# A transformer layer's sparse experts on one core: loads held back, unread products in a gap, and token weights computed later

## The chip, the cores and the metric

The kernel runs on one core of one Trainium2 chip. The metric is the device time of one execution in microseconds, taken as the median of several runs. A time "at 505.30" is microseconds from the start of the profiled span. TensorE's clock has two levels here, 1.2 and 2.4 GHz; the profile gives the granted clock as a share of the higher one, so 0.50 is the lower level and 1.00 the higher.

## The reference

Two layers (`DEPTH = 2`) over 512 tokens of width 1024, float32. Each has a token mixer (attention) and then a sparse mixture of 16 experts, of which every token uses two. The change lies in the experts:

```
def _moe(h, w_router, router_bias, w_gate, w_up, w_down):
    scores = jax.nn.sigmoid((t @ w_router).astype(jnp.float32))
    sel = scores + router_bias.astype(jnp.float32)
    grp_score = jnp.sum(lax.top_k(sel.reshape(-1, N_GROUPS, EXPERTS_PER_GROUP), TOP_K)[0], -1)
    best = jnp.argmax(grp_score, axis=-1)
...
    _, idx = lax.top_k(jnp.where(in_group, sel, -jnp.inf), TOP_K)
    top_s = jnp.take_along_axis(scores, idx, axis=-1)
    gate = top_s / jnp.sum(top_s, -1, keepdims=True)
    combine = jnp.sum(jax.nn.one_hot(idx, N_EXPERTS, dtype=jnp.float32) * gate[..., None], 1)
    hg = jnp.einsum('td,edf->tef', t, w_gate)
    hu = jnp.einsum('td,edf->tef', t, w_up)
    act = jax.nn.silu(hg) * hu * combine[..., None].astype(t.dtype)
    y = jnp.einsum('tef,efd->td', act, w_down)
```

`w_gate` and `w_up` are 1024x256 for each expert, `w_down` 256x1024.

## The kernel before, in words

The instructions of each engine stand in one fixed order, in which the engine runs them; waits between engines are semaphores that the framework puts in. `tc.issue_after(x)` puts what is built inside it behind instruction x in that order. Loads are asked for on SP's queue unless another engine is named, and a load waits until its tile's last reader is done.

**Products.** A float32 product is made of three passes over split operands: H is the operand rounded to the matmul format (a cast on ScalarE, `wH`, L215), L the rest (a subtraction on VectorE, `wL`, L216), and TensorE adds H·H, L·H and H·L (L225 to L227). `wH` and `wL` have six buffers each (`NWH`), each holds 128x512 and serves six products of 128x256.

**The router.** For each layer the last norm of the mixer gives `h` (512 tokens); its four 128-row tiles go to `h2d` in DRAM, three from SP's queue and the last from ScalarE's (L996). VectorE ranks the scores in many small operations; small matmuls count positions (`pos`) and turn the ranking into lists of token rows (`mp`, L1088). `vt` (L1093) holds the row numbers that the gathers and scatters use. Then VectorE computes the token weights: `rt_tmp`, `posf`, `rt_den`, `rt_gt` (L1098 to L1106) and, in `keep_weights`, `rt_we` (L1207 to L1210) and `ae` (L1214), which TensorE transposes (L1215) into `G`, for the last two experts (`NKEEP`).

**The experts.** For each expert e, in order: `x_load` gathers its up to 128 token rows from `h2d` into `xe` by an indirect DMA on POOL (L1119); `x_split` transposes them on TensorE (eight of 128x128, L330) and splits them into `xH` (ScalarE, L337) and `xL` (VectorE, L338); `x_gate` makes 24 products and a silu (`ea`, L1144), `x_up` 24 more; `x_down` (L1188) is issued one expert later, behind the next gate, and its result `ye` is scattered by POOL (L1193). `overflow()` stands between the first gather and the first split: a branch that all engines take and whose body runs only if an expert has more than 128 tokens.

**What is loaded ahead.** `AHEADW` lists twelve weight tiles of 1 MB, those of experts 0 to 3. The first `HOLD` of them are asked for on SP early, from the end of the mixer on, as their buffers come free; the others on POOL, behind gather 0. Before the change HOLD is 10: only (3, up) and (3, down) wait for the gather. The three `xes` are the gathers' buffers, which ScalarE clears (L1028) once in each layer.

Of the kernel before, what the change touches and what calls it, by code (L numbers as in the profile page):

```python
# [13 lines left out]
OP = mybir.AluOpType  # L14
# [73 lines left out]
def build(tc, A, out):  # L88
    nc = tc.nc
    with ExitStack() as es:  # L90
# [90 lines left out]
        xdr = dr.tile([S, D], F32, name="xdr")  # L181


        def wraw(src, shape, tag="raw", eng=SY):
            if tag in ("f4", "row"):
                n = 1024 // shape[1]
                raws = [(fp if tag == "f4" else rp).tile([P, n] + shape[1:], F32, tag=tag, name="raw4") for _ in range(shape[0] // n)]
                for i, raw in enumerate(raws):
                    eng.dma_start(raw, src[:, i * n:(i + 1) * n])
                return lambda s: raws[s.start // n][:, s.start % n:s.start % n + s.stop - s.start]  # L190
            raw = wp.tile([P] + shape, F32, tag="raw", name="raw", bufs=NRAW) if tag == "raw" else e8("raw8", shape)
            eng.dma_start(raw, src)
# [107 lines left out]
        def stats(src):  # L300
            st = small("st", [2, 6])
            for i in range(2):
                V.bn_stats(st[:, i, :], parts(src, i * 512, (i + 1) * 512)[0][0])
            mv = small("mv", [2])
            V.bn_aggr(mv, st.rearrange("p a b -> p (a b)"))
            r = pool_rsqrt("rstd", mv[:, 1:2], LN_EPS, 1)
            nb = small("nb", [1])
            PO.tensor_scalar(nb, mv[:, 0:1], r, -1.0, op0=OP.mult, op1=OP.mult)
            return mv[:, 0:1], r, nb

        issued = {}

        def norm(src, name, g, b, st=None):

            m, r, nb = st or stats(src)
            n = f4(name, [D])
            for lo, hi in ((0, 256), (256, D)):
                for p, z in parts(src, lo, hi):
                    V.scalar_tensor_tensor(n[:, z], p, m, g[:, z], op0=OP.subtract, op1=OP.mult)
            V.scalar_tensor_tensor(n, n, r, b, op0=OP.mult, op1=OP.add)  # L320
            return n

        def plain(src, dst, st=None):

            m, r, nb = st or stats(src)
            ACT.activation(dst, src, AF.Identity, bias=nb, scale=r)

        def turn(dst, src):
# [93 lines left out]
        def layer(l, hH, hL, W0, after=None, qk=None):  # L422
# [660 lines left out]
            for k in range(2):  # L1083
                for t in range(NT):
                    at = ats[:, NT * k + t]
                    V.tensor_scalar(at, iotab, sv[:, 0, k, t:t + 1], None, op0=OP.is_equal)
                    for i in range(2):
                        PE.matmul(mp, lhsT=at, rhs=src[:, NT * k + t, 2 * i:2 * i + 2], start=(k == 0 and t == 0 and i == 0),  # L1088
                                  stop=(k == 1 and t == NT - 1 and i == 1))
            cnti = small("cnti", [1], I32, bufs=1)  # L1090
            V.tensor_reduce(cnti, pos[:, NT, :], axis=X, op=OP.max)
            vt = small("vt", [2, NE], I32, bufs=1)
            order1 = V.tensor_tensor(vt, ct["none"].rearrange("p (i e) -> p i e", i=2), mp, op=OP.subtract)  # L1093
            vidx, tidx = vt[:, 0], vt[:, 1]
# [7 lines left out]
            den = rt("den", [NT])
            V.tensor_add(den, sv[:, 1, 0, :], sv[:, 1, 1, :])
            V.reciprocal(den, den)
            gt = rt("gt", [2, NT])
            V.tensor_mul(gt, sv[:, 1], den[:, None, :].to_broadcast([P, 2, NT]))  # L1106
            gm = rt("gm", [2, NT])
            V.tensor_scalar(gm, sv[:, 0], float(CAP), None, op0=OP.is_lt)
# [15 lines left out]
            def x_split(e):  # L1124
                xe = XE.pop(e)
                xH = f4("xH", [8, P], F32R)
                xL = f4("xL", [8, P], F32R)
                for q in range(2):
                    p = ptp([P, 4, P])
                    transposes(lambda i: xe[:, (4 * q + i) * P:(4 * q + i + 1) * P], p, 4)  # L1130
                    split_ps(p, xH[:, 4 * q:4 * q + 4, :], xL[:, 4 * q:4 * q + 4, :])
                XS[e] = xH, xL

            def x_prod(e, w):
                xH, xL = XS[e]
# [147 lines left out]
                            V.tensor_copy(oi[:, 0:n], sh[:, 0:n])  # L1283

            for e in range(AHEAD):
                i = x_load(e)
                if e == 0:
                    first = i
            with tc.issue_after(first.ins):
                for e, w, tag in AHEADW[HOLD:]:  # L1290
                    PRE[e, w] = wraw(x_src(e, w), x_shape(w), tag, PO)
            overflow()
            x_split(0)
            for e in range(NE):
                if e + AHEAD < NE:
                    x_load(e + AHEAD)
                if e == EKEEP:
                    keep_weights()
                x_gate(e)
                if e > 0:  # L1300
                    x_down(e - 1)
                x_up(e)
                if e + 1 < NE:
                    x_split(e + 1)
            ys = []
            for t in range(NT):
                for k in range(2):
# [106 lines left out]
```

## Time and profile before

| | |
|---|---|
| median of 3 runs | 1373.92 us (1373.52 to 1374.74) |
| the profiled execution's own time | 1374.85 us |
| its span | 1373.1 us |
| mean granted TensorE clock over the span | 0.961 |
| TensorE busy | 1262.8 us (92%) |
| VectorE busy | 1031.9 us (75%) |
| ScalarE busy | 704.5 us (51%) |
| GpSimd (POOL) busy | 157.5 us (11%) |
| moved by DMA | 263.59 MB, mean 192 GB/s |

The profiled execution is one of the kernel's executions, 0.93 us above the median; 1.75 us of its time lie outside the span. Busy shares are averages over stages with different limits: of the table TensorE's 92% tells only that the other 8% are where it stands still. The experts of layer 1 begin at about 499 us, those of layer 2 at about 1162 us.

### The profile page before, as it was taken

The page shows a single profiled execution, that of the slowest core. Times are in us where ns is not written, and L with a number is a line of the kernel's source. Part 1 is how long each engine was busy: PE and PEld are TensorE (multiplying, and loading weights), DVE is VectorE, ACT ScalarE, POOL GpSimd, SP SyncE. Part 2 cuts the span into 40 slices and gives each one's busy share as a digit, 9 for nine tenths or more (in the row PEclk, how much of TensorE's full clock was granted, in tenths as well). Part 3 has the DMA queues.
Part 4 walks back from the last instruction along what each step waited for, and adds up shares of the span by engine and source line. Part 5 has one row for each costly group of instructions (what it writes and reads, how often), then busy time and mean ns, then how long its engine had stood idle before and what let it go on. Part 6 is the DMA issues. An engine that isn't in the chain of part 4 may idle for free.

```text
span 1373.1 us, 21373 instructions
## 1 busy us (share of the span) xinstructions
PE 1262.8 (92%) x7925; PEld 1027.6 (75%) x7925; DVE 1031.9 (75%) x2104; ACT 704.5 (51%) x1460; POOL 157.5 (11%) x161
## 2 busy tenths in 40 slices
PE   4898999999999949999969899999999994999996
PEld 3787777677778948888648777777777794788883
DVE  4877788776368879999886888564325978799997
ACT  2344444556644157777434454455556413777760
POOL 1032000000000222222020300000000012222210
PEclk9799999999999969999988999999999997899999
DMA  9747544455156187999643365112123546889963
GB/s 309 235 138 292 174 152 166 149 189 184 62 170 224 59 303 261 311 336 342 249 157 131 114 224 177 46 60 70 50 77 111 179 156 218 274 281 342 351 221 136
DMA packets 181070, 263.59 MB, mean 192 GB/s; under 512 B 18281, under 2 KB 131337, under 8 KB 180960
## 3 DMA queue, kind: packets, MB, share of 16 engines
q1 hardware_dynamic: 157104, 221.27, 47.8%
q0 software_dynamic: 11456, 24.07, 5.0%
q10 hardware_dynamic: 12400, 16.83, 3.8%
q8 instruction: 64, 1.05, 0.3%
q14 instruction: 46, 0.38, 0.1%
HBM read 250.79 MB, written 27.30 MB: 203 GB/s over the span
## 4 chain that ended last, share of the span: by engine, by line
PE 32%; DVE 10%; ACT 2%; issue 2%; DMA 2%; POOL 1%; SPq 1%; POOLq 0%; DVEq 0%; ACTq 0%
PE mm L225 5%; PE mm L226 5%; PE mm L227 5%; DVE wL L216 5%; PE mm L1188 3%; PE tp L330 2%; PE av L668 1%; PE y L1321 1%; ACT wH L215 1%; POOL rs L286 1%; PE mo L226 1%; PE mo L227 1%; PE mo L225 1%; PE s L634 1%; DMA raw<-in_w_exp_down 1%
## 5 line engine op out<-in xcount | busy, mean ns | idle before, releaser
L216 DVE TENSOR_TENSOR wL<-raw,wH 128x512 fp32r<-128x512 f32 x520 | 339.7, 685 | 94.4 <-ACT wH L215 80.6
L215 ACT CAST wH<-raw 128x512 fp32r<-128x512 f32 x520 | 318.4, 622 | 163.5 <-PE mm L1188 45.9
L225 PE MATMUL mm<-hH,wH 128*128 128x512 f32 x544 | 219.3, 403 | 0.0
L226 PE MATMUL mm<-hL,wH 128*128 128x512 f32 x544 | 217.9, 400 | 0.0
L227 PE MATMUL mm<-hH,wL 128*128 128x512 f32 x544 | 216.1, 397 | 0.0
L225 PE MATMUL mm<-wH,xH 128*128 128x256 f32 x512 | 149.1, 291 | 2.6 <-DVE yk L1189 1.6
L227 PE MATMUL mm<-wH,xL 128*128 128x256 f32 x512 | 148.6, 290 | 1.0 <-DVE xL L338 1.0
L226 PE MATMUL mm<-wL,xH 128*128 128x256 f32 x512 | 146.4, 286 | 0.3 <-DVE wL L216 0.3
L226 PEld LDWEIGHTS mm<-hL,wH 128*128 128x128 f32 x544 | 103.4, 190 | 21.9 <-issue 2.1
L225 PEld LDWEIGHTS mm<-hH,wH 128*128 128x128 f32 x544 | 103.2, 190 | 21.8 <-issue 0.8
L227 PEld LDWEIGHTS mm<-hH,wL 128*128 128x128 f32 x544 | 103.4, 190 | 21.2 <-issue 0.7
L249 DVE SCALAR_TENSOR_TENSOR acc<-araw,cond,acc 128x512 f32<-128x512 f32 x148 | 110.5, 747 | 5.7 <-DMA araw<-in_w_ada 3.0
L225 PEld LDWEIGHTS mm<-wH,xH 128*128 128x128 f32 x512 | 98.8, 193 | 5.5 <-DVE yk L1189 2.5
L226 PEld LDWEIGHTS mm<-wL,xH 128*128 128x128 f32 x512 | 98.6, 193 | 2.4 <-DVE wL L216 1.2
L227 PEld LDWEIGHTS mm<-wH,xL 128*128 128x128 f32 x512 | 98.2, 192 | 2.3 <-DVE xL L338 1.8
L286 POOL TENSOR_TENSOR rstd<-rstd,c_mhalf 128x1 f32<-128x1 f32 x32 | 20.4, 637 | 478.1 <-DVE rstd L285 478.1
L642 ACT ACTIVATE pp<-s,nm,rs 128x512 f32<-128x512 f32 x64 | 49.7, 778 | 33.0 <-DVE nm L639 31.3
L1188 PE MATMUL mm<-raw,eT 128*128 128x512 f32 x128 | 63.3, 617 | 3.6 <-ACT eT L1171 1.5
L225 PE MATMUL mm<-wH,hH 128*128 128x256 f32 x192 | 58.7, 308 | 5.4 <-ACT hH L406 3.6
L227 PE MATMUL mm<-wH,hL 128*128 128x256 f32 x192 | 57.2, 303 | 1.6 <-DVE hL L372 1.4
L1193 POOL DMA_INDIRECT y<-ye,vt x28 | 33.6, 1199 | 210.1 <-DVE ye L1189 210.1
L226 PE MATMUL mm<-wL,hH 128*128 128x256 f32 x192 | 56.7, 299 | 0.0
(303 smaller groups left out, 2655.7 us busy)
## 6 DMA issues: line engine op xcount, KB each, us to landing
araw<-in_w_ada SPq DMA_DIRECT2D x44, 1024.0 KB, 5.4
raw<-in_w_in SPq DMA_DIRECT2D x40, 1024.0 KB, 5.1
raw<-in_w_exp_gate SPq DMA_DIRECT2D x32, 1024.0 KB, 9.1
raw<-in_w_exp_up SPq DMA_DIRECT2D x28, 1024.0 KB, 11.1
raw<-in_w_exp_down SPq DMA_DIRECT2D x28, 1024.0 KB, 9.4
raw<-in_w_out SPq DMA_DIRECT2D x8, 1024.0 KB, 5.3
y<-y SPq DMA_DIRECT2D x16, 512.0 KB, 8.1
eraw<-in_w_ada SPq DMA_DIRECT2D x4, 1024.0 KB, 13.8
```

The lines of the kernel that those rows point to most:

```text
L215: ACT.copy(H, raw(s))
L216: V.tensor_sub(L, raw(s), H.bitcast(F32))
L225: PE.matmul(o, lhsT=lH, rhs=rH, start=(i == 0), stop=False)
L226: PE.matmul(o, lhsT=lH, rhs=rL, start=False, stop=False)
L227: PE.matmul(o, lhsT=lL, rhs=rH, start=False, stop=(i == n - 1))
L249: last = V.scalar_tensor_tensor(acc, raw[:, k, :], ck, acc, op0=OP.mult, op1=OP.add)
L286: PO.tensor_tensor(r, r, mhalf[:, :n], op=OP.pow)
L330: return PE.transpose(dst, src, ident[0:k, 0:k])
L634: PE.matmul(s, lhsT=qT[h // 4][:, h % 4, tcols(t)], rhs=kTH[:, kv, :], start=True, stop=False)
L642: ACT.activation(pp, s, AF.Exp, bias=nm, scale=rs, accum_out=dn)
L1188: PE.matmul(p, lhsT=a, rhs=w, start=(i == 0), stop=(i == len(todo) - 1))
L1193: st = PO.indirect_dma_start(out=y2, out_offset=bass.IndirectOffsetOnAxis(ap=vidx[:, e:e + 1], axis=0), in_=ye, in_offset=None, bounds_che ...
```

## The change

Four things change, and one small one besides.

1. HOLD goes from 10 to 4. Only (0, gate), (0, up), (0, down) and (1, gate) are asked for early. The other eight tiles, in the same order, are asked for on SP behind the branch of `overflow()` (`load_held`). Ahead of the first of them ScalarE copies one column of `mp` into its tile, so that the DMA, which writes the same tile, waits for the copy and so for `mp`; the second half of that weight and the rest follow.
2. Seven matmuls of 128x512 (`idle`, bfloat16) that nobody reads are put on TensorE behind the last matmul of `mp`, ahead of expert 0's transposes.
3. The token weights (`token_weights`) and `keep_weights` are built behind the last `xL` of expert 1's rows instead of right behind `vt`.
4. With that the scheduler places the last `h2d` tile's DMA on ScalarE behind one more clearing of an `xe` buffer.

The small one: `nb`, a scalar per token that only `plain` needs, is computed there and no longer in each `stats`. Line numbers after the change are a few higher than before: `ae` is L1222 instead of L1214, its transposes L1223 instead of L1215, the products L229 to L231 instead of L225 to L227.

```
+            with tc.issue_after(last.ins):
+
+                idle = pat([P, 512], "idle")
+                for i in range(NIDLE):
+                    last = PE.matmul(idle, lhsT=oneb, rhs=ats[:, 0:4], start=(i == 0), stop=(i == NIDLE - 1))
+            warm = last
...
-            with tc.issue_after(order1.ins):
+            def token_weights():
+
                 V.tensor_mul(tmp, o12, sco[:, None].to_broadcast([P, 2, NT, NE]))
-                posf = rt("posf", [NT + 1, NE])
                 V.tensor_copy(posf, pos)
-            V.reduce_sum(sv[:, 1], tmp, axis=X)
...
+                V.reduce_sum(sv[:, 1], tmp, axis=X)
...
             for e in range(AHEAD):
-                i = x_load(e)
-                if e == 0:
-                    first = i
-            with tc.issue_after(first.ins):
+                x_load(e)
+
+            def load_held():
+
+                hold = None
                 for e, w, tag in AHEADW[HOLD:]:
-                    PRE[e, w] = wraw(x_src(e, w), x_shape(w), tag, PO)
+                    with ExitStack() as order:
+                        if hold is not None:
+                            order.enter_context(tc.issue_after(hold.ins))
+                        PRE[e, w] = wraw(x_src(e, w), x_shape(w), tag, first=None if hold else lambda z: ACT.copy(z, mp[:, 0, 0:1]))
+                    hold = hold or issued["load"]
+
             overflow()
-            x_split(0)
+            load_held()
+            with tc.issue_after(warm.ins):
+                split1 = x_split(0)
             for e in range(NE):
                 if e + AHEAD < NE:
                     x_load(e + AHEAD)
                 if e == EKEEP:
-                    keep_weights()
+                    with tc.issue_after(split1.ins):
+                        token_weights()
+                        keep_weights()
...
                 if e + 1 < NE:
-                    x_split(e + 1)
+                    i = x_split(e + 1)
+                    split1 = i if e == 0 else split1
...
-HOLD = 10
+HOLD = 4
+NIDLE = 7
```

VectorE behind `vt`, before the change: the token weights and the first four `rt_we` operations, then the branch of `overflow()` (`cnti`).

```order
L1093 TENSOR_TENSOR vt<-c_none,mp 128x32
L1098 TENSOR_TENSOR rt_tmp<-rt_o_4912,rt_sco 128x128
L1100 COPY rt_posf<-pos 128x80
L1101 TENSOR_REDUCE rt_sv<-rt_tmp 128x8
L1103 TENSOR_TENSOR rt_den<-rt_sv 128x4
L1104 RECIPROCAL rt_den<-rt_den 128x4
L1106 TENSOR_TENSOR rt_gt<-rt_sv,rt_den 128x8
L1207 TENSOR_TENSOR rt_we<-rt_o_4912,rt_gt 128x8
L1208 TENSOR_TENSOR rt_we<-rt_we,rt_gm 128x8
L1209 TENSOR_TENSOR rt_gt<-rt_gt,rt_we 128x8
L1210 TENSOR_TENSOR rt_we<-rt_we 128x4
L1220 TENSOR_LOAD cnti
```

After the change the branch follows `vt` at once, and these operations stand among the subtractions of experts 1 and 2. VectorE's order from right behind the last subtraction of (2, gate), over the four of (2, up), which read raw_5084, to the second group of `ae`:

```order
L1217 TENSOR_TENSOR rt_gt<-rt_gt,rt_we 128x8
L220 TENSOR_TENSOR wL<-raw_5084,wH 128x512
L1218 TENSOR_TENSOR rt_we<-rt_we 128x4
L220 TENSOR_TENSOR wL<-raw_5084,wH 128x512
L1222 TENSOR_SCALAR ae<-iotab,rt_posf,rt_we 128x128 x4
L220 TENSOR_TENSOR wL<-raw_5084,wH 128x512
L1215 TENSOR_TENSOR rt_we<-rt_o_4880,rt_gt 128x8
L220 TENSOR_TENSOR wL<-raw_5084,wH 128x512
L1216 TENSOR_TENSOR rt_we<-rt_we,rt_gm 128x8
L1217 TENSOR_TENSOR rt_gt<-rt_gt,rt_we 128x8
L1218 TENSOR_TENSOR rt_we<-rt_we 128x4
L1222 TENSOR_SCALAR ae<-iotab,rt_posf,rt_we 128x128 x4
```

Before the change the first group of `ae` stood in ones and a pair among expert 1's subtractions, the second ahead of the last subtraction of (2, gate).

TensorE at the transposes of `ae`, before: the second group of four stands between products of (2, gate), each of which has other products around it (the first group of four stands 16 products earlier).

```order
L1215 MATMUL tp<-c_ident,ae 128x128
L226 MATMUL mm<-wL,xH 128x256
L1215 MATMUL tp<-c_ident,ae 128x128
L227 MATMUL mm<-wH,xL 128x256
L1215 MATMUL tp<-c_ident,ae 128x128
L225 MATMUL mm<-wH,xH 128x256
L1215 MATMUL tp<-c_ident,ae 128x128
L330 MATMUL tp<-c_ident,ea 128x128 x2
```

After: all eight stand in one piece behind the 24 products of (2, gate), with the transposes of expert 1's `ea` among them and down(1) (L1196) behind.

```order
L229 MATMUL mm<-wH,xH 128x256
L230 MATMUL mm<-wL,xH 128x256
L231 MATMUL mm<-wH,xL 128x256
L1223 MATMUL tp<-c_ident,ae 128x128 x5
L331 MATMUL tp<-c_ident,ea 128x128 x2
L1223 MATMUL tp<-c_ident,ae 128x128 x3
L1196 MATMUL mm<-raw_5078,eT 128x512
```

SP behind the branch, after the change: the held loads, raw_5073 (the tile that ScalarE's copy writes) second among them. Before the change all of these but raw_5090, raw_5092 and raw_5093 stood ahead of the branch, and those three on POOL.

```order
L1230 UNCONDITIONAL_BRANCH
L193 DMA raw_5074<-in_w_exp_up 128x4x256
L193 DMA raw_5073<-in_w_exp_up 128x4x256
L193 DMA raw_5078<-in_w_exp_down 128x1024
L193 DMA raw_5079<-in_w_exp_down 128x1024
L196 DMA raw_5082<-in_w_exp_gate 128x8x256
L196 DMA raw_5084<-in_w_exp_up 128x8x256
L196 DMA raw_5086<-in_w_exp_down 128x2x1024
L196 DMA raw_5088<-in_w_exp_gate 128x8x256
L196 DMA raw_5090<-in_w_exp_up 128x8x256
L193 DMA raw_5092<-in_w_exp_down 128x1024
L193 DMA raw_5093<-in_w_exp_down 128x1024
```

## Rows read from the trace of the kernel before

**Rows 1.** The page's first part, TensorE with its share.

```profile
PE 1262.8 (92%) x7925; PEld 1027.6 (75%) x7925; DVE 1031.9 (75%) x2104; ACT 704.5 (51%) x1460; POOL 157.5 (11%) x161
```

**Rows 2.** Windows, start of layer 1's experts: length, busy us, clock, DMA share, GB/s.

```profile
480.00:490.00 10.00, 4.59 (x35) 3.94 (x34) 9.52 (x18) 2.49 (x4) 1.94 (x4) 0.78 1.01 358
490.00:500.00 10.00, 1.89 (x30) 1.47 (x29) 9.30 (x48) 6.68 (x8) 1.29 (x2) 0.50 0.99 325
500.00:510.00 10.00, 4.71 (x22) 4.29 (x23) 5.40 (x12) 3.86 (x7) 6.62 (x7) 0.52 0.59 183
510.00:520.00 10.00, 9.06 (x75) 8.57 (x73) 8.42 (x15) 8.76 (x16) 1.38 (x1) 1.00 0.93 336
```

**Rows 3.** Timeline, layer 1: start, length, engine, line, operation, idle time and its releaser.

```profile
498.50 0.19 DVE L1093 TENSOR_TENSOR vt<-c_none,mp 128x32 int32<-128x32 f32 x1 [0.25 <-PE mp L1088]
...
500.48 0.16 DVE L1210 TENSOR_TENSOR rt_we<-rt_we 128x4 f32<-128x4 f32 x1
...
500.64 1.17 POOL L1119 DMA_INDIRECT xe<-h2d,vt  x1 [9.25 <-DVE rt_we L1210]
501.81 1.90 DVE L216 TENSOR_TENSOR wL<-raw,wH 128x512 fp32r<-128x512 f32 x3 [1.17 <-DVEq L1222]
...
505.30 1.94 PE L330 MATMUL tp<-c_ident,xe 128*128 128x128 f32 x8 [6.83 <-DMA xe<-h2d,vt]
```

**Rows 4.** DMA tables of 490:532, of 1150:1195 and of 455:476: median to landing.

```profile
h2d<-h ACTq DMA_DIRECT2D x1, 512.0 KB, 7.0
xe<-h2d,vt POOLq DMA_INDIRECT x6, 7.0
...
xe<-h2d,vt POOLq DMA_INDIRECT x6, 5.7
...
h2d<-h SPq DMA_DIRECT2D x2, 512.0 KB, 3.6
```

**Rows 5.** Timeline, layer 2, the same place.

```profile
1162.12 0.19 DVE L1093 TENSOR_TENSOR vt<-c_none,mp 128x32 int32<-128x32 f32 x1 [0.25 <-PE mp L1088]
...
1164.22 1.16 POOL L1119 DMA_INDIRECT xe<-h2d,vt  x1 [9.22 <-DVE rt_gt L1209]
...
1168.85 1.94 PE L330 MATMUL tp<-c_ident,xe 128*128 128x128 f32 x8 [6.76 <-DMA xe<-h2d,vt]
```

**Rows 6.** Timeline of VectorE, layer 1, 512 to 536.

```profile
513.62 0.69 DVE L216 TENSOR_TENSOR wL<-raw,wH 128x512 fp32r<-128x512 f32 x1 [1.51 <-PE mm L227]
...
528.98 1.11 DVE L1214 TENSOR_SCALAR ae<-iotab,rt_posf,rt_we 128x128 f32<-128x128 bf16 x4
```

**Rows 7.** Timeline of ScalarE and its queue, layer 1, 492 to 499.

```profile
492.70 0.35 ACTq L996 DMA_DIRECT2D h2d<-h  x1
493.10 2.95 ACT L1028 ACTIVATE xe<-row 128x1024 f32<-128x1024 f32 x3 [0.67 <-DVE rt_duo L1048]
497.35 1.28 ACT L215 ACT_TABLE_LOAD   x1 [1.30 <-ACTq L1222]
```

**Rows 8.** Waits of TensorE, 480 to 548: what for, total us, times, longest.

```profile
PE mm L225 <- ACT xH L337: 0.5, 1, 0.5
PE mm L227 <- DVE xL L338: 0.5, 1, 0.5
PE mm L1188 <- ACT eT L1171: 0.2, 1, 0.2
PE mm L226 <- DVE wL L216: 0.2, 1, 0.2
```

**Rows 9.** Timeline of ScalarE, the silu of experts 1 and 2.

```profile
519.58 0.39 ACT L1144 ACTIVATE ea<-mm 128x256 f32<-128x256 f32 x1
531.63 0.38 ACT L1144 ACTIVATE ea<-mm 128x256 f32<-128x256 f32 x1 [0.25 <-PE mm L227]
```

**Rows 10.** Timeline of TensorE, two products that follow each other at the low clock.

```profile
508.38 0.41 PE L226 MATMUL mm<-wL,xH 128*128 128x256 f32 x1
508.59 0.41 PE L227 MATMUL mm<-wH,xL 128*128 128x256 f32 x1
```

More of the change, by code (lines that the diff above doesn't have):

```diff
@@ L181, in build, with wraw @@
         xdr = dr.tile([S, D], F32, name="xdr")
-        def wraw(src, shape, tag="raw", eng=SY):
+        issued = {}
+        def wraw(src, shape, tag="raw", eng=SY, first=None):
             if tag in ("f4", "row"):
@@ L188, in wraw @@
                 for i, raw in enumerate(raws):
-                    eng.dma_start(raw, src[:, i * n:(i + 1) * n])
+                    if first is not None and not i:
+                        first(raw[:, 0, 0:1])
+                    issued["load"] = eng.dma_start(raw, src[:, i * n:(i + 1) * n])
                 return lambda s: raws[s.start // n][:, s.start % n:s.start % n + s.stop - s.start]
             raw = wp.tile([P] + shape, F32, tag="raw", name="raw", bufs=NRAW) if tag == "raw" else e8("raw8", shape)
-            eng.dma_start(raw, src)
+            issued["load"] = eng.dma_start(raw, src)
             return lambda s: raw[:, s]
@@ L305, in stats @@
             V.bn_aggr(mv, st.rearrange("p a b -> p (a b)"))
[L306 to L311, printed above, removed]
+            return mv[:, 0:1], pool_rsqrt("rstd", mv[:, 1:2], LN_EPS, 1)
         def norm(src, name, g, b, st=None):
-            m, r, nb = st or stats(src)
+            m, r = st or stats(src)
             n = f4(name, [D])
@@ L323, in plain @@
         def plain(src, dst, st=None):
-            m, r, nb = st or stats(src)
+            m, r = st or stats(src)
+            nb = small("nb", [1])
+            PO.tensor_scalar(nb, m, r, -1.0, op0=OP.mult, op1=OP.mult)
             ACT.activation(dst, src, AF.Identity, bias=nb, scale=r)
@@ L1087, in layer @@
                     for i in range(2):
-                        PE.matmul(mp, lhsT=at, rhs=src[:, NT * k + t, 2 * i:2 * i + 2], start=(k == 0 and t == 0 and i == 0),
-                                  stop=(k == 1 and t == NT - 1 and i == 1))
+                        last = PE.matmul(mp, lhsT=at, rhs=src[:, NT * k + t, 2 * i:2 * i + 2], start=(k == 0 and t == 0 and i == 0),
+                                         stop=(k == 1 and t == NT - 1 and i == 1))
+            with tc.issue_after(last.ins):
[3 more added lines that the diff above has]
+            warm = last
             cnti = small("cnti", [1], I32, bufs=1)
@@ L1094, in layer @@
             vidx, tidx = vt[:, 0], vt[:, 1]
-            with tc.issue_after(order1.ins):
+            posf, gt, gm = rt("posf", [NT + 1, NE]), rt("gt", [2, NT]), rt("gm", [2, NT])
+            def token_weights():
                 V.tensor_mul(tmp, o12, sco[:, None].to_broadcast([P, 2, NT, NE]))
-                posf = rt("posf", [NT + 1, NE])
                 V.tensor_copy(posf, pos)
-            V.reduce_sum(sv[:, 1], tmp, axis=X)
[L1102 to L1108, printed above, removed]
+                V.reduce_sum(sv[:, 1], tmp, axis=X)
+                den = rt("den", [NT])
+                V.tensor_add(den, sv[:, 1, 0, :], sv[:, 1, 1, :])
+                V.reciprocal(den, den)
+                V.tensor_mul(gt, sv[:, 1], den[:, None, :].to_broadcast([P, 2, NT]))
+                V.tensor_scalar(gm, sv[:, 0], float(CAP), None, op0=OP.is_lt)
             r_g2 = row_load(moddr[l, 5])
@@ L1130, in x_split @@
                     transposes(lambda i: xe[:, (4 * q + i) * P:(4 * q + i + 1) * P], p, 4)
-                    split_ps(p, xH[:, 4 * q:4 * q + 4, :], xL[:, 4 * q:4 * q + 4, :])
+                    i = split_ps(p, xH[:, 4 * q:4 * q + 4, :], xL[:, 4 * q:4 * q + 4, :])
                 XS[e] = xH, xL
+                return i
             def x_prod(e, w):
```

## The prediction

> **What bounds the kernel now.** Read first TensorE's share on the page [rows 1]: it is busy 92% of the span, so time is won only where it stands still, or lost where it is made to. Then the windows over the start of the experts, layer 1 [rows 2]: in the three stretches of 10 us from 480 to 510 TensorE works 4.59, 1.89 and 4.71, at a granted clock of 0.78, 0.50 and 0.52 of full; from 510 to 520 it works 9.06 at 1.00. So the place of the change is some 30 us long, and occurs once in each of the two layers. The DMA share beside it is 1.01 and 0.99 until 500, and 0.59 from 500 to 510.
>
> The timeline [rows 3] shows what is waited for. `vt`, the row numbers for the gathers, is ready at 498.50 + 0.19 = 498.69, but gather 0 issues on POOL only at 500.64. The releaser printed, `rt_we`, is not read by the gather; what is late is the last tile of `h2d`, the tensor whose rows are gathered. It was asked for at 492.70 [rows 7] and takes 7.0 us to land [rows 4], 499.70, among weight loads at a share of 1. The two `h2d` tiles before it, on an emptier DMA, took 3.6 (the last row there). The gathered rows arrive, and TensorE begins to transpose, at 505.30, 4.66 us after the issue. Layer 2 repeats it [rows 5]: `vt` done at 1162.31, gather 1164.22, transposes 1168.85 (4.63 later).
>
> From there VectorE is the tight engine: in 510 to 520 it is busy 8.42 of 10, and of its idle 1.58 us 1.51 are one wait, until 513.62, for TensorE to free a weight buffer [rows 6]. TensorE in turn waits just a little for its neighbours in the first experts: 0.5, 0.5, 0.2 and 0.2 [rows 8]. From the silu of expert 1 to that of expert 2 it takes 531.63 - 519.58 = 12.05 us [rows 9]; this cycle carries the transposes of the kept weights (`ae`).
>
> **Part by part, for one layer.**
>
> *Loads held back, gather earlier.* With 8 MB not yet asked for, the last `h2d` tile meets an almost empty DMA. It is issued behind one `xe` memset more (2.95 for three, 0.98 us each, [rows 7]), so at about 493.7. Landing in 3.6 us it is there at 497.3, before `vt`. The gather then follows `vt`, say at 499.0 (an estimate: its end and 0.3 for the signal) instead of 500.64; in layer 2 at 1162.6 instead of 1164.22. I take -1.65.
>
> But the held loads leave at the same moment. The ScalarE copy that the first of them waits for stands behind a table load that ends at 497.35 + 1.28 = 498.63 [rows 7]; so SP asks for 8 MB from about 499 on, more than two full windows carry (358 GB/s are 3.6 MB in 10 us). The DMA tables of the first 40 us of either layer's experts [rows 4], in which most transfers ran at a share near 1, give gathers 7.0 and 5.7 us to land, median of six each. Half way, 6.35, is 1.7 above the 4.65 of today's gather in the empty DMA. Bounds: 0, and 7.0 - 4.65 = 2.35. Net for the rows of expert 0: -1.65 + 1.7 = +0.05, between -1.65 and +0.7.
>
> By the Trainium skill (DMA: Bandwidth & Descriptors, Issuing engines are not separate DMA queues) transfers of all issuers interleave on the same 16 engines; by that rule the gather on POOL's queue is not spared because the loads sit on SP's, and the net would be at the upper end. The 7.0 us of the `h2d` tile on ScalarE's queue, beside loads on SP's, agrees with it.
>
> The weights themselves should come in time. All eight tiles at 325 to 358 GB/s are in by 499 + 25 = 524, in the order in which they are used, and the first, (1, up), is split only behind the rows of expert 1, well after 513.62 [rows 6]. Cost 0; if the cover fails, see rival 4.
>
> *Unread products.* Products of 256 columns repeat every 0.21 us at the low clock (508.38, 508.59, [rows 10]), so 512 columns take some 0.43 (an estimate from these), seven 3.0: about 498.5 to 501.5, inside the wait, cost 0. Then TensorE stands again for 3 us or more until the rows. What they could give: at the high clock the eight transposes would take half of 1.94 [rows 3], and the products between 507 and 509.5, twelve at 0.21, half of 2.5: 0.97 + 1.25 = 2.2 per layer. The windows give the clock full for 0.56 of 480 to 490 (0.78 is 0.56 at full and the rest at half), which is some 4 us past the last dense products, and half from there until 509.6 (0.52). Nothing in the trace shows that seven products raise it, and that it outlasts the pause behind them. I take 0, bounds -2.2 and 0.
>
> *Token weights later.* Ten small operations, from 498.69 to 500.64 [rows 3], and `gm` lay in a wait of VectorE that ended only at 501.81; they cost nothing. Without them six `wL` instead of three can run ahead of the rows, but VectorE then stands at the buffers anyway, as until 513.62. In the new place they stand in the tight stretch, and both groups of four `ae` come behind subtractions of (2, up). On TensorE all eight `ae` transposes follow straight behind the 24 products of (2, gate), ahead of down(1). From the last subtraction of (2, gate) to the last `ae` VectorE has four `wL` (0.61 each: 1.90 for three that overlap by 0.07), eight `ae` (four in 1.11, [rows 6], 1.0 without the tail) and six small operations (0.12 each, an estimate from their 0.16 less overlap): 2.4 + 2.0 + 0.7 = 5.1 us. TensorE already waits for a subtraction in this place (0.2, [rows 8]), so VectorE has no lead there. Meanwhile TensorE has the last six products (0.7) and ten transposes (eight `ae`, two `ea`, 0.12 each at the high clock, half of 1.94/8, 1.2): 5.1 - 1.9 = 3.2 us of standing, less the last 0.2 that it stands for a subtraction now: **+3.0**. Bounds: 0 (VectorE has a lead of 3 us), and 4.0 (the 0.5 and 0.5 that the rows of expert 1 wait for, once more at expert 3, whose eight transposes now come in one piece).
>
> *`nb`* is taken from POOL behind the `rstd` that the others wait for: 0.
>
> Sum: 0.05 + 3.0 = 3.05 per layer, 6.1 for two. The profiled execution took 1374.85 (span 1373.1 and 1.75 around it), so 1380.95; it lies 0.93 above the median of 1373.92, so **1380.0**. Within 0.2% (2.75 us) a measurement of this kernel can't tell a change from none.
>
> **Rivals.**
> 1. *The clock is up when the rows come.* Place 498 to 509.6 and its like; -2.2 per layer, -4.4: 1375.6, the same. For: the seven products fill what was idle, and the clock outlived the last dense products by some 4 us. Against: 3 us of standing behind them. It turns into a gain once the standing at `ae` is below some 0.8 us a layer. By the Trainium skill (TensorE: Matmul & The Clock Gate, What's actually happening) "the default state is throttled, and activity releases the throttle"; the half-speed rows after the long wait agree, a release by so few products no run here shows.
> 2. *VectorE gets ahead* (the other side). Three subtractions done earlier (1.9 us) outweigh the moved token work (1.95). Then neither `ae` nor the waits of 0.5, 0.5, 0.2 and 0.2 stop TensorE: 0.05 - 1.4 = -1.35 per layer: 1374.85 - 2.7 - 0.93 = 1371.2. It decides from a lead of 3 us at the end of (2, gate). For: six casts and subtractions now fit in ahead of the rows. Against: the wait until 513.62 at the buffers, where any lead is capped at six tiles. With the quiet gather on top 1368.
> 3. *The gather starts no earlier.* If `h2d`, issued 1 us later, still takes 7.0, the gather follows it 1 us later: 1.0 + 1.7 + 3.0 = 5.7 per layer: 1385.3. Against: the loads that made it 7.0 are gone.
> 4. *Weights late.* 8 MB in 25 us, with gathers among them, leave (2, down) and (3, gate) the least room. If TensorE stands 2 us a layer for one of them, 1384.
>
> **Numbers.** Chances: forecast 0.5; rival 1 0.14; rival 2 0.24; rival 3 0.05; rival 4 0.07. Faster comes from half of rival 2, a third of rival 1, and the forecast's lower edge with a quiet gather and a short wait (0.05): 0.22; the same from the rest of 1 and 2 and another 0.05: 0.26; slower 0.52. The forecast's own range is 1377 to 1383.5 (per layer +1.5 to +4.7). The range of 8 in 10 reaches to rival 2 and to 4: 1370.5 to 1384.5.
>
> **What would show it.** Gather 0 issued near 499 and its rows 6 us or more later; expert 0's transposes between 504 and 506, still at 0.50; idle time of 2 to 3.4 us ahead of `tp<-ae` put down to VectorE; the silu cycle of expert 1 to 2 at 14 to 15.5 instead of 12.05. The prediction is wrong if the clock at 505 reads 1.00, if the `ae` waits are under 1 us, if `h2d` still holds the gather, or if a later cycle is stretched by a wait for a weight's DMA.

## The result, and the profile after

The change made the kernel slower, and by two and a half times as much as the sum said (15.0 us, where it had 6.1): median 1389.13 us (1388.1 to 1392.17, 4 runs) against 1374.12 us (4 runs of the kernel before beside them), a ratio of 1.0120 (95% interval 1.0107 to 1.0132). The result lies outside the predicted range of 1370.5 to 1384.5, whose middle forecast was 1380.0. The profiled execution was the slowest of the four: 1392.17 us, span 1390.4.

The windows of the kernel after, at the places of [rows 2] and ten microseconds beyond (length, busy us of TensorE, its weight loads, VectorE, ScalarE and POOL, then the granted clock, DMA share, GB/s):

```profile
490.00:500.00 10.00, 3.09 (x33) 1.99 (x34) 8.39 (x41) 6.48 (x9) 0.55 (x2) 0.50 0.14 55
500.00:510.00 10.00, 2.97 (x11) 1.81 (x10) 3.52 (x6) 2.57 (x6) 3.02 (x3) 0.67 1.03 348
510.00:520.00 10.00, 9.54 (x73) 8.87 (x71) 7.08 (x12) 8.49 (x15) 1.98 (x2) 0.92 1.03 361
...
530.00:540.00 10.00, 7.25 (x34) 5.21 (x34) 7.45 (x23) 4.92 (x10) 1.46 (x1) 0.77 0.81 265
```

The DMA share has changed places: 0.14 instead of 0.99 until 500, 1.03 instead of 0.59 behind it. And a second hole has opened, from 530 to 540, where TensorE works 7.25 us and the clock is at 0.77. The kernel before worked on there, at 1.00:

```profile
530.00:540.00 10.00, 9.76 (x64) 8.04 (x63) 9.17 (x17) 7.48 (x15) 1.92 (x2) 1.00 0.75 239
```

The first hole in the timeline, beside [rows 3] and [rows 7]:

```profile
492.81 0.35 ACTq L997 DMA_DIRECT2D h2d<-h  x1
...
498.63 0.19 DVE L1100 TENSOR_TENSOR vt<-c_none,mp 128x32 int32<-128x32 f32 x1 [0.33 <-PE mp L1089]
498.64 0.95 SPq L193 DMA_DIRECT2D raw<-in_w_exp_up  x2
498.81 2.68 PE L1095 MATMUL idle<-ats,oneb 128*128 128x512 bf16 x6 [0.22 <-issue]
...
499.70 1.14 POOL L1126 DMA_INDIRECT xe<-h2d,vt  x1 [9.45 <-ACT wH L219]
...
508.52 1.94 PE L331 MATMUL tp<-c_ident,xe 128*128 128x128 f32 x8 [7.03 <-DMA xe<-h2d,vt]
```

The gather issues 0.94 us earlier than in [rows 3], as the edit to the loads was said to do, but SP began to ask for the held 8 MB 1.06 us ahead of it. Its rows come 8.82 us after the issue instead of 4.66, so expert 0 begins 3.2 us later than before. In layer 2, beside [rows 5], it is 9.93 us instead of 4.63:

```profile
1172.72 1.62 POOL L1126 DMA_INDIRECT xe<-h2d,vt  x1 [9.38 <-ACT wH L219]
...
1182.65 1.94 PE L331 MATMUL tp<-c_ident,xe 128*128 128x128 f32 x8 [7.99 <-DMA xe<-h2d,vt]
```

The second hole, in TensorE's timeline: the eight `ae` transposes behind the products of (2, gate), and down(1) behind them.

```profile
533.60 1.01 PE L1223 MATMUL tp<-c_ident,ae 128*128 128x128 f32 x4 [0.85 <-DVE ae L1222]
536.51 0.45 PE L1223 MATMUL tp<-c_ident,ae 128*128 128x128 f32 x1 [1.90 <-DVE ae L1222]
...
537.84 3.78 PE L1196 MATMUL mm<-raw,eT 128*128 128x512 f32 x4
```

TensorE stands 0.85 and 1.90 us for VectorE, at the place that the prediction named. What it did not name comes behind that: the last row's four matmuls take 3.78 us. In the kernel before they took 1.98:

```profile
532.33 1.98 PE L1188 MATMUL mm<-raw,eT 128*128 128x512 f32 x4 [0.24 <-ACT eT L1171]
```

Finer windows of this kernel show why, and show the unread products too:

```profile
500.00:502.00 2.00, 1.49 (x4) 0.30 (x2) 1.02 (x2) 0.42 (x2) 0.90 (x2) 0.68 0.97 299
502.00:504.00 2.00, 0.00 (x0) 0.00 (x0) 1.73 (x3) 1.79 (x4) 1.70 (x2) 1.00 1.08 342
504.00:506.00 2.00, 0.00 (x0) 0.00 (x0) 0.77 (x2) 0.00 (x0) 0.43 (x1) 0.67 1.01 373
506.00:508.00 2.00, 0.00 (x0) 0.00 (x0) 0.00 (x0) 0.00 (x0) 0.00 (x0) 0.50 1.02 362
...
534.00:536.00 2.00, 0.61 (x3) 0.28 (x2) 1.91 (x7) 0.87 (x2) 0.00 (x0) 0.85 0.93 314
536.00:538.00 2.00, 1.49 (x7) 1.30 (x7) 1.11 (x4) 0.58 (x2) 0.00 (x0) 0.50 0.90 272
...
542.00:544.00 2.00, 2.00 (x13) 1.75 (x12) 1.01 (x3) 1.23 (x2) 0.00 (x0) 0.94 1.06 343
```

In layer 1 the clock rose behind the seven products: it is at 1.00 from 502 to 504, when TensorE has nothing to do, and back at 0.50 before the rows are there. In layer 2 of the same execution it stayed at 0.50, with six of the seven products on record in this window:

```profile
1172.00:1182.00 10.00, 2.66 (x6) 0.65 (x5) 3.79 (x6) 3.31 (x7) 3.82 (x3) 0.50 0.95 305
```

At 534 to 536, with the standing at `ae`, the clock falls once more, until shortly after 542, so that most of down(1) runs at 1.2 GHz. From its first matmul to the first product behind it down(1) takes 5.34 us instead of 3.21; in layer 2, where the clock is back before 1216, it takes 4.14. The silus on ScalarE (beside [rows 9]) give the sum of the second hole:

```profile
522.25 0.38 ACT L1152 ACTIVATE ea<-mm 128x256 f32<-128x256 f32 x1
535.13 0.39 ACT L1152 ACTIVATE ea<-mm 128x256 f32<-128x256 f32 x1
551.09 0.39 ACT L1152 ACTIVATE ea<-mm 128x256 f32<-128x256 f32 x1
```

The silu of expert 3 in the kernel before:

```profile
541.99 0.38 ACT L1144 ACTIVATE ea<-mm 128x256 f32<-128x256 f32 x1
```

From expert 1's to expert 3's it takes 28.84 us; before it took 22.41 (541.99 - 519.58). The products of (2, gate) stand ahead of the `ae` transposes on TensorE, so most of the loss shows in the cycle of expert 2 to 3, 15.96, and not in that of 1 to 2, 12.88, where the prediction put it (14 to 15.5).

### The profile page after: what moved, and what is told of

It reads as the page before. It is cut to its first block, busy times and chain, and to the rows that moved or that the text cites. A ratio compares the mean times of both kernels' runs of the same rounds, so it can differ in the third digit from the quotient of the medians.

```text
span 1390.4 us, 21398 instructions
## 1 busy us (share of the span) xinstructions
PE 1271.6 (91%) x7937; PEld 1029.1 (74%) x7939; DVE 1032.3 (74%) x2104; ACT 705.2 (51%) x1462; POOL 136.7 (10%) x131
## 4 chain that ended last, share of the span: by engine, by line
PE 29%; DVE 13%; ACT 3%; issue 2%; DMA 2%; POOL 1%; POOLq 0%; DVEq 0%; ACTq 0%; SPq 0%
PE mm L230 5%; PE mm L231 5%; PE mm L229 5%; DVE wL L220 5%; PE mm L1196 3%; PE tp L331 2%; PE av L669 1%; DVE st L307 1%; ACT wH L219 1%; POOL rs L290 1%; DMA xe<-h2d,vt 1%; PE mo L230 1%; PE mo L231 1%; PE mo L229 1%; PE s L635 1%
## 5 line engine op out<-in xcount | busy, mean ns | idle before, releaser
L229 PE MATMUL mm<-hH,wH 128*128 128x512 f32 x544 | 219.0, 403 | 0.0
L231 PE MATMUL mm<-hH,wL 128*128 128x512 f32 x544 | 215.9, 397 | 0.0
L229 PE MATMUL mm<-wH,xH 128*128 128x256 f32 x512 | 148.6, 290 | 2.8 <-DVE yk L1197 1.7
L231 PE MATMUL mm<-wH,xL 128*128 128x256 f32 x512 | 147.3, 288 | 0.9 <-DVE xL L339 0.7
L229 PEld LDWEIGHTS mm<-hH,wH 128*128 128x128 f32 x544 | 103.0, 189 | 21.6 <-issue 0.8
L231 PEld LDWEIGHTS mm<-hH,wL 128*128 128x128 f32 x544 | 103.2, 190 | 21.2 <-issue 0.7
L229 PEld LDWEIGHTS mm<-wH,xH 128*128 128x128 f32 x512 | 98.3, 192 | 6.1 <-ACT xH L338 2.5
L231 PEld LDWEIGHTS mm<-wH,xL 128*128 128x128 f32 x512 | 97.6, 191 | 2.4 <-DVE xL L339 1.3
L1196 PE MATMUL mm<-raw,eT 128*128 128x512 f32 x128 | 66.0, 640 | 4.5 <-ACT eT L1179 2.5
L229 PE MATMUL mm<-wH,hH 128*128 128x256 f32 x192 | 57.7, 302 | 6.0 <-ACT hH L407 3.6
L231 PE MATMUL mm<-wH,hL 128*128 128x256 f32 x192 | 56.0, 297 | 1.6 <-DVE hL L373 1.4
```

Of the source, the lines that this page charges most:

```text
L229: PE.matmul(o, lhsT=lH, rhs=rH, start=(i == 0), stop=False)
L231: PE.matmul(o, lhsT=lL, rhs=rH, start=False, stop=(i == n - 1))
L1196: PE.matmul(p, lhsT=a, rhs=w, start=(i == 0), stop=(i == len(todo) - 1))
```

## The experiments

Ten kernels. On the chips of these runs the kernel before spread from 1368 to 1379 us, so a median tells a couple of microseconds at best, and the traces, of one execution each, tell more of where the time goes. This table is worked out from each kernel's timeline, layer 1 / layer 2, in us: from gather 0's issue to the first transpose of its rows; from the end of `vt` to expert 0's silu; from expert 1's silu to expert 3's; what the twelve cycles from expert 3 to 15 take above 12 x 10.36; and from the end of `vt` to expert 15's silu.

| kernel | gather to transposes | `vt` to silu 0 | silu 1 to 3 | later cycles, excess | `vt` to silu 15 |
|---|---|---|---|---|---|
| before | 4.66 / 4.63 | 14.00 / 14.77 | 22.41 / 22.41 | 0 / 0 | 167.62 / 168.50 |
| after | 8.82 / 9.93 | 16.64 / 18.43 | 28.84 / 27.61 | 0 / 0 | 176.53 / 177.08 |
| e1_tokens_early | 9.17 / 8.49 | 17.58 / 16.27 | 22.42 / 22.42 | 0 / 0 | 171.14 / 169.80 |
| e2_hold_11 | 4.44 / 4.89 | 14.97 / 14.64 | 27.84 / 27.83 | 0 / 0 | 173.82 / 173.58 |
| e3_no_idle | 7.20 / 10.05 | 15.69 / 18.62 | 27.60 / 27.68 | 0 / 0 | 174.48 / 177.45 |
| e4_loads_behind_rows | 4.85 / 5.09 | 12.84 / 14.13 | 29.15 / 27.93 | 0 / 0 | 172.97 / 173.07 |
| e5_early_rows | 4.53 / 4.79 | 13.35 / 12.66 | 22.40 / 22.74 | 1.0 / 4.0 | 167.78 / 170.50 |
| e6_early_rows_no_idle | 4.58 / 5.01 | 12.94 / 12.97 | 22.41 / 22.48 | 3.0 / 5.2 | 169.42 / 171.70 |
| e7_early_rows_idle16 | 4.89 / 4.70 | 12.56 / 12.28 | 22.43 / 22.41 | 1.1 / 1.5 | 167.16 / 167.32 |
| e8_later_transposes | 8.36 / 10.09 | 16.52 / 18.72 | 25.40 / 25.41 | 0 / 0 | 173.06 / 175.25 |
| e9_before_idle22 | 4.91 / 4.54 | 13.61 / 13.22 | 22.43 / 22.42 | 0 / 0 | 168.29 / 166.81 |
| e10_hold7_rows_idle16 | 4.59 / 4.44 | 12.25 / 12.05 | 22.42 / 22.39 | 0 / 0 | 165.79 / 165.52 |

**e1_tokens_early.** The token weights back behind `vt`, `keep_weights` without its order:

```
-            def token_weights():
+            with tc.issue_after(order1.ins):
                 V.tensor_mul(tmp, o12, sco[:, None].to_broadcast([P, 2, NT, NE]))
                 V.tensor_copy(posf, pos)
...
+            V.reduce_sum(sv[:, 1], tmp, axis=X)
...
-                    with tc.issue_after(split1.ins):
-                        token_weights()
-                        keep_weights()
+                    keep_weights()
```

> The changed kernel with the token weights put back right behind vt and the ae work back among the products; held loads and unread products stay. Theory A (TensorE standing at the ae transposes, and the clock that falls there, is the larger part of the loss): in the changed kernel's trace the two silu cycles from expert 1 to 3 take 28.8 and 27.6 us in the two layers against 22.4 before, together 11.6 us; they come back, so 1377.5 (1376 to 1381), no idle over 0.5 us ahead of an ae transpose, clock 1.00 from 513 on. Theory B (the loads beside the first gather are the loss, the wait at ae only shifts work): less than 3 us come back, 1386 to 1389.

Measured 1379.64 (10 runs), ratio to before 1.0037 (1.0017 to 1.0056), inside theory A's range. The silus of experts 1 to 3 stand where they stood before, 12.06 and 10.36 us apart:

```profile
524.08 0.39 ACT L1151 ACTIVATE ea<-mm 128x256 f32<-128x256 f32 x1
536.14 0.39 ACT L1151 ACTIVATE ea<-mm 128x256 f32<-128x256 f32 x1 [0.25 <-PE mm L231]
546.50 0.39 ACT L1151 ACTIVATE ea<-mm 128x256 f32<-128x256 f32 x1
```

The place of the token weights cost 6.4 and 5.2 us; the late rows remain in this kernel (9.17 and 8.49).

**e2_hold_11.**

```
-HOLD = 4
+HOLD = 10
```

(Of the two tiles then left the first, (3, up), is of a kind that the copy does not tie, so it goes out early too, as the eleventh.)

> The changed kernel with HOLD 10, where eleven of the twelve tiles are asked for ahead of the branch and only (3, down) behind it; unread products and late token weights stay. Theory A: the wait at ae stays whole (1.0 and 1.9 us, cycle of expert 2 to 3 at 15 to 16 us); only the later rows come back, 2.7 + 4.2 = 6.9 us, so 1382 (1380 to 1384). Theory B: nearly all comes back, 1374 to 1377. Either way expert 0's rows come some 4.7 us behind the gather's issue instead of 8.8.

Measured 1384.44 (6 runs), 1.0071 (1.0039 to 1.0103), just above the upper edge of A's range. The gather takes 4.44 and 4.89 us again; the loss between silu 1 and 3 stays, 27.8. The two costs are separate: each of e1 and e2 takes one away and leaves the other. The gather issues 2.2 and 1.5 us after `vt` here, 0.9 and 0.8 in the kernel after. This fits loads that, asked for early, hold up `h2d` as they did before; its landing is not recorded in this trace.

**e3_no_idle.**

```
-            with tc.issue_after(last.ins):
-
-                idle = pat([P, 512], "idle")
-                for i in range(NIDLE):
-                    last = PE.matmul(idle, lhsT=oneb, rhs=ats[:, 0:4], start=(i == 0), stop=(i == NIDLE - 1))
...
-NIDLE = 7
+NIDLE = 0
```

> The changed kernel without the seven unread products. The trace of the changed kernel shows the clock at 1.00 only from some 501 to 505, before the rows are there. Theory: they are worth nothing, 1389 within 1.5 us, and the clock stays 0.50 from 490 until some 3 us of products are through. Rival: they help, because the clock's next rise comes sooner for them: then 2 to 4 us slower, 1391 to 1393.

Measured 1387.37 (4 runs), 1.0100 (1.0055 to 1.0145): 1.8 us under the kernel after, and its four runs, from 1384.5 to 1391.6, overlap with that kernel's. The rival (2 to 4 us slower) doesn't show. The gather's transfer alone differs by 3 us between the layers of this run (7.20 and 10.05), so that a microsecond can't be read from it. e5 and e6 take the question up again.

**e4_loads_behind_rows.**

```
-                        PRE[e, w] = wraw(x_src(e, w), x_shape(w), tag, first=None if hold else lambda z: ACT.copy(z, mp[:, 0, 0:1]))
+                        PRE[e, w] = wraw(x_src(e, w), x_shape(w), tag, first=None if hold else lambda z: ACT.copy(z, XS[0][0].bitcast(F32)[:, 0, 0:1]))
...
-            load_held()
             with tc.issue_after(warm.ins):
                 split1 = x_split(0)
+            load_held()
```

> The changed kernel with the held loads waiting for a copy of a column of expert 0's xH instead of mp, so that gather 0 runs in an empty DMA; the rest as in the change. Theory (the loads beside the gather cost 4.2 and 5.3 us of its transfer): rows 4.7 us behind the issue, at about 504.4 in layer 1, 9 us less in all: 1380 (1378 to 1383), with the wait at ae unchanged. Rival (weights now late, asked for 7 us later than in the change): TensorE waits for casts or DMA at experts 1 to 3 and the gain is gone, 1387 or more.

Measured 1382.36 (9 runs), 1.0061 (1.0043 to 1.0079), inside the theory's range. With the held loads still to come the gather needs 4.85 and 5.09 us. POOL's timeline of e4, and TensorE's:

```profile
501.03 1.14 POOL L1126 DMA_INDIRECT xe<-h2d,vt  x1 [9.45 <-DVEq L1230]
```

```profile
505.88 1.77 PE L331 MATMUL tp<-c_ident,xe 128*128 128x128 f32 x8 [3.03 <-DMA xe<-h2d,vt]
```

From `vt` to silu 0 it takes 12.84 and 14.13 us, less than before. So what delayed the rows were the held loads that set out beside the gather. The loss between silu 1 and 3 remains.

**e8_later_transposes.**

```
                     for t in range(NT):
                         V.tensor_scalar(a[:, t], iotab, posf[:, t, e:e + 1], we[:, 0, t:t + 1], op0=OP.is_equal, op1=OP.mult)
-                        PE.transpose(p[:, t], a[:, t], ident)
-                    ACT.copy(G[:, i], p)
+                    AE.append(a)
...
                     x_down(e - 1)
+                if e == EKEEP:
+                    with tc.issue_after(PEL[e - 1].ins):
+                        turn_weights()
```

`turn_weights` makes the eight transposes and the two copies; `PEL` holds the last matmul of a down.

> The changed kernel with only the eight ae transposes and the copies to G moved behind down(1); VectorE's order and all loads as in the change. In the changed kernel's trace TensorE stands 2.75 us at ae in layer 1, and the clock is 0.50 from about 535.7 to 542. Theory (standing and falling clock together make the loss): down(1) fills the wait, the clock does not fall, some 4 to 5 us a layer come back: 1380 (1378.5 to 1382). Rival (only the standing counts): 1.7 us a layer come back, 1385.7. Second rival (VectorE's extra work, not TensorE's order, is what costs): nothing comes back, 1389.

Measured 1386.68 (6 runs), 1.0088 (1.0066 to 1.0111). The theory was right on the clock and wrong on the size; by time alone the median lies nearest to the first rival (1385.7). The stretch from 528 to 546 in e8:

```profile
528.00:546.00 18.00, 14.84 (x103) 12.53 (x103) 16.80 (x42) 11.94 (x22) 5.28 (x4) 1.00 0.87 294
```

In the kernel after the same stretch has a clock of 0.81:

```profile
528.00:546.00 18.00, 15.25 (x83) 11.83 (x82) 12.79 (x36) 9.66 (x18) 3.72 (x3) 0.81 0.87 287
```

Without the fall of the clock, and with down(1) ahead of the transposes, 3.4 and 2.2 us of the 6.4 and 5.2 are back. But 3.0 us per layer remain, and TensorE's timeline of e8 shows most of them:

```profile
535.02 1.98 PE L1196 MATMUL mm<-raw,eT 128*128 128x512 f32 x4 [1.30 <-ACT eT L1179]
...
538.46 0.50 PE L1196 MATMUL mm<-wH,eL 128*128 128x512 f32 x1 [0.99 <-DVE eL L339]
```

First TensorE waits 1.30 us for `eT`, the copy of expert 1's transposed `ea`, which stands behind the silu of expert 2 in ScalarE's order (534.32 and 534.60): with the `ae` transposes gone from this place nothing of TensorE's is left to fill that wait. Then it waits 0.99 us for `eL`, which stands behind both groups of `ae` on VectorE. Layer 2 has the same two waits. To move the transposes alone could not get past the other engines' orders.

**e5_early_rows and e6_early_rows_no_idle.** e5 has the edits of e1 and e4 together; e6 is e5 without the unread products.

> Both repairs together: the held loads wait for expert 0's xH, and the token weights and ae are where they were before the change; HOLD 4 and the seven unread products stay. If the two costs found so far (the loads beside the first gather, the standing at ae) are independent and are all, this lies at 1382.4 - (1387.4 - 1379.6 to 1389.1 - 1379.6) = 1373 to 1374.6, less nothing else: equal to before, or some 1.4 us under it, because the gather issues about 1.1 us after vt instead of 2.0 in each layer: 1372.5. Rival (a third cost, such as weights that are asked for 7 us later than before): 1377 or more, with waits for casts at experts 1 to 3.

> The run e5 without the seven unread products. If they are worth nothing, as the traces suggest (the clock they raise falls again before the rows come), the same as e5 within 1 us. If the clock's rise after the rows does come sooner for them, 2 us slower than e5.

Measured 1377.97 (12 runs), 1.0027 (1.0006 to 1.0049), and 1377.90 (12 runs), 1.0027 (1.0011 to 1.0043). The medians show no worth of the seven products, but the 12 runs of either kernel scatter over 12 us and more, so they could not tell the 2 us of the other case either. The two traces are sharper: from the first transpose to silu 0 it takes 7.94 and 7.06 us with the products, 7.46 and 7.12 without. And e5's rival is right that there is a third cost, though not where it put it (experts 1 to 3). Both repairs work (first column and third as before), but now cycles of later experts, most of them from 9 to 13, are stretched, up to 12.60 us. ScalarE's waits in e6, layer 2, 1225 to 1325 (in all, times, longest):

```profile
ACT wH L219 <- DMA raw<-in_w_exp_gate: 4.3, 4, 1.4
ACT wH L219 <- DMA raw<-in_w_exp_down: 3.7, 1, 3.7
ACT wH L219 <- DMA raw<-in_w_exp_up: 0.6, 3, 0.2
```

Neither the kernel before nor that after has a row of this kind between 560 and 675. The held loads put some 8 MB of transfers off, and the DMA has little room to make up for it. Its share in layer 1 from 560 to 660, before the change:

```profile
560.00:660.00 100.00, 99.19 (x652) 84.40 (x651) 91.69 (x154) 76.83 (x145) 21.46 (x17) 1.00 0.92 314
```

In the kernel after there is no room left. No cast waits for a weight there; that TensorE, some 9 us late itself, gave the loads their time is the likely reason (e1, 3 us late, has no stretched cycle either), and no run isolates it:

```profile
560.00:660.00 100.00, 99.19 (x653) 84.47 (x652) 91.71 (x155) 76.92 (x145) 21.60 (x18) 1.00 1.00 340
```

**e7_early_rows_idle16.** e5 with

```
-NIDLE = 7
+NIDLE = 16
```

> The run e5 with 16 unread products instead of seven, so that they last until the rows come. Theory (the products only lack length): clock 1.00 at the transposes of expert 0, transposes 1 us and first products 1.2 us faster in each layer: 4.4 us under e5, 1368. Rival (the clock does not rise in time, 16 products at 0.43 us last 6.9 us and hold up the rows by 1.5 us in each layer): 3 us above e5, 1375.5.

Measured 1373.34 (12 runs), 1.0001 (0.9982 to 1.0020); e5 beside it 1377.97. That is 4.6 us less, near the theory's 4.4, but runs that scatter over 12 us and more leave open how much of it is real. TensorE's timeline of e7:

```profile
496.92 5.87 PE L1095 MATMUL idle<-ats,oneb 128*128 128x512 bf16 x16
503.08 1.06 PE L331 MATMUL tp<-c_ident,xe 128*128 128x128 f32 x8 [0.30 <-DMA xe<-h2d,vt]
```

Sixteen products last until the rows come, and the eight transposes take 1.06 us instead of 1.94: the clock is up. From the first transpose to silu 0 it takes 6.78 us in both layers, 0.3 to 1.2 us less than in e5 and e6; that is what these traces give the longer filler, and the match with 4.4 us is in part luck (less late weights in layer 2 make 2.5 us of the difference to e5). The gain against before from `vt` to silu 0 is 1.44 and 2.49 us, 0.8 and 1.0 of it rows that are there earlier; the late weights take 1.1 and 1.5 back (ScalarE's wait for a gate's DMA in layer 1: 1.4 us).

**e9_before_idle22.** The kernel before with 22 unread products behind `mp` (the same lines as in the change), its loads and token weights untouched.

```
 HOLD = 10
+NIDLE = 22
```

> The kernel before with one part of the change alone, in another length: 22 unread products on TensorE behind mp, which last until the rows come (in e7 16 lasted 5.0 to 5.9 us, so 22 last some 6.3 to 7.2, from 498.7 to 505 or 506). Loads, token weights and all else as before. Theory (the lead of the weights is kept, the clock is up when the rows come): transposes 1.0 us and the products behind them 1.2 us or more faster in each layer, 4 us or more less: 1369 to 1370, all later silu cycles 10.36. Rival (the products, some of them at the low clock, last past the rows): up to 1 us given back per layer, 1371 to 1372.

Measured 1371.66 (12 runs), 0.9985 (0.9971 to 1.0000). The number is the rival's, the cause another. In layer 2 1.7 us are gained, in layer 1 not. There TensorE, which is earlier and has four of the transposes of expert 2's rows higher up in its order than before (behind 7 products of (1, gate) instead of 24), meets the gather of these rows, which stands behind 2 MB of loads in POOL's queue.

```profile
517.41 0.63 PE L330 MATMUL tp<-c_ident,xe 128*128 128x128 f32 x4 [0.94 <-DMA xe<-h2d,vt]
```

**e10_hold7_rows_idle16.** e7 with three more tiles asked for early, and the copy's tie for the first held tile of any kind:

```
-HOLD = 4
+HOLD = 7
...
             raw = wp.tile([P] + shape, F32, tag="raw", name="raw", bufs=NRAW) if tag == "raw" else e8("raw8", shape)
+            if first is not None:
+                first(raw[:, 0, 0:1])
```

> The run e7 with three more tiles asked for early (HOLD 7: expert 1's up and down and expert 2's gate; five wait for the rows). In e5, e6 and e7 silu cycles of experts 9 to 13 were stretched to 10.5 to 12.6 us, which I take for weights that come late because 8 MB were asked for some 20 us later. Theory: with 3 MB more in time the stretched cycles shrink by half or more (e7 lost 1.1 us in layer 1 and 1.7 in layer 2 so), while the gather still runs alone: 1 to 2 us under e7 in the sum from vt to the last silu, 165.5 to 166.5 per layer. Rival (they are stretched by something else, as the order of SP's loads): no change against e7's 167.2.

Measured 1367.95 (1366.19 to 1368.56, 6 runs), 0.9949 (0.9931 to 0.9968): 5.5 us faster than the kernel before beside it, the only clear gain, and from `vt` to silu 15 as the theory said. Of the 1.8 and 3.0 us that the traces give it there against before, 1.1 and 1.3 are rows that are there earlier and 0.6 and 1.5 lie between the first transpose and silu 0. No cast waits for a weight from 560 to 665, the DMA has room again:

```profile
560.00:660.00 100.00, 99.18 (x652) 84.42 (x651) 91.76 (x154) 77.11 (x145) 21.55 (x17) 1.00 0.94 323
```

and the clock is up when the rows arrive:

```profile
500.54 4.45 PE L1097 MATMUL idle<-ats,oneb 128*128 128x512 bf16 x15 [0.22 <-DVE vt L1102]
506.02 1.06 PE L333 MATMUL tp<-c_ident,xe 128*128 128x128 f32 x8 [1.03 <-DMA xe<-h2d,vt]
```

## Why the prediction was wrong

The sign was right, and both causes of the loss were named; two terms of the sum were far too small. From `vt` to expert 15's silu the kernel after is 8.9 us longer in layer 1 and 8.6 in layer 2, which is all of the 17.3 us between the two spans.

- *Loads held back, gather earlier.* `h2d` no longer holds the gather, as forecast: it issues 0.9 and 0.8 us after `vt` instead of 2.0 and 1.9, a gain of 1.1 (I had estimated 0.3 after `vt` and so 1.65). The step that failed is the price of company, +1.7 with a bound of +2.35: measured 8.82 - 4.66 = 4.2 and 9.93 - 4.63 = 5.3. I took it from medians over all gathers of the first 40 us [rows 4], and a median hides what was to be priced. One by one, the third and the sixth of the gathers that layer 1's median was taken from:

```profile
xe<-h2d,vt POOLq DMA_INDIRECT x1, 11.7
...
xe<-h2d,vt POOLq DMA_INDIRECT x1, 4.6
```

The first of these was asked for at 505.79, straight behind 2 MB of loads, the other at 527.23. The trace of before thus held gathers at 11.7, 11.6, 10.8 and 10.5 us beside others at 4.4 to 4.6. (The four slow ones stood behind loads in POOL's own queue; the gather of the kernel after does not, its loads are on SP's.) The rule of the Trainium skill that was weighed there (DMA: Bandwidth & Descriptors, Issuing engines are not separate DMA queues) pointed to the upper end, and the trace went beyond even that. e4 shows the cause, by taking the company away: 4.85 and 5.09. Expert 0's silu was 2.6 and 3.7 us later than before, where the term was +0.05. The 3.6 us for `h2d` was read from the first two tiles, not from the two ahead of the last: the third, asked for at 482.45 among loads, took 6.7. With the loads held the last tile did land fast, 2.6 us in e8.
- *Token weights later*, +3.0 with a bound of 4.0: measured 6.4 and 5.2. e1 shows that it is the place of this work and nothing else. The standing of TensorE was sized well (2.75 us in two waits in either layer, 3.2 forecast before what it replaces). What failed is that the sum priced the standing alone and put the clock that falls in it at nothing. By the traces down(1) takes 2.1 and 0.9 us more than before, and this is most of the difference between the layers: the clock is at 0.50 from about 535.5 to 542 in layer 1 and comes back before 1216 in layer 2. The other 1.5 us of either layer lie among the products and transposes ahead of down(1), some of them at 0.50 as well, and at expert 3; they were not taken apart. In e8, where the clock holds 1.00, 25.4 us are needed instead of 28.8 and 27.6; it moved the transposes as well, so its 3.4 and 2.2 us are not the clock's alone. Of the 3.0 that stay there 1.30 are the wait for `eT` and 0.99 that for `eL`.
- *The tight engine.* The prediction calls VectorE tight from 510 on. Its own row [rows 2] gives TensorE 9.06 of those 10 us and VectorE 8.42, and VectorE's one wait there is for TensorE. VectorE's extra work cost so much because TensorE had to wait for its result.
- *Unread products* at 0: right, but for a reason that I had not seen whole. In the six kernels with seven of them the clock rose behind them in eight of the twelve layers, but fell again in the pause before the rows or, once (e4, layer 1), as they came; in the other four it stayed at 0.50 until after the rows (rival 1 asked for the clock). e5 against e6: no difference that could be told. In e7, e9 and e10, where 16 to 22 last until about the time when the rows come, it is up at the rows in all six layers: rival 1's mechanism is real, and the length was what lacked.
- *Weights late* (rival 4, 0.07): not in the kernel after. The wait appeared as soon as the other two losses were repaired (e5, e6), 1 to 5 us per layer, and went when three tiles were asked for early (e10: no cycle is stretched).
- *VectorE gets ahead* (rival 2, 0.24) did not happen; from 500 to 530 it waits 5.7 us for ScalarE's `xH`, behind the late rows, and 4.5 for its `wH` instead. `nb` at 0: no run isolated it.

That the kernel after scatters by 4 us in its four runs was not followed up; the gather's transfer (7.20 to 10.09 us where the loads run beside it) and the time for which the clock falls (5.34 or 4.14 us for down(1)) vary from layer to layer by enough to allow for it.

## What to carry to other kernels

Whatever is held back to keep a small urgent transfer alone must wait for that transfer's arrival, not for the condition under which it is issued too; and only as much may be held as the DMA's free share later on can make up for. To price such a transfer among others, look at single transfers that met the same company, not at a median. Work that costs nothing in a wait costs its full time, and what queues behind it, where another engine waits for its result. A wait of TensorE should be priced with the clock that it loses: look up the granted clock in the same stretch of a variant without the wait, and let a filler last until the awaited data come, or leave it out.

## What the runs showed of the hardware

Behind seven unread products of 512 columns (2.68 us for the six that the profile has) the granted clock of layer 1 rose from 0.50 to 1.00 by 502; it stayed there over some 3 us in which TensorE did nothing, and fell before 506. The same seven left it at 0.50 in layer 2 (1172 to 1182). Around the 2.75 us of standing at `ae`, two waits with four transposes between, it fell to 0.50 for some 6 us of work in layer 1 (535.5 to 542) and for less in layer 2. By the Trainium skill (TensorE: Matmul & The Clock Gate, HAM oscillation — how this bites in real kernels) a long enough wait for a DMA between groups of matmuls makes the next group start at the low clock; the rows at 534 to 542 agree, with two waits on VectorE, 0.85 and 1.90 us, in place of one on a DMA. A 512 KB gather that set out 1 to 1.5 us after SP had begun to ask for 8 MB took 7.2 to 10.1 us from its issue to the first transpose of its rows, against 4.4 to 5.1 where those loads came later or long before, in the layers of these runs.
